# Table building of layer 0 queued behind the first norm's modulation, half of that norm's scaling on VectorE, byte masks

## The chip, the cores and the metric

The kernel runs on one core of a Trainium2 chip. The metric is device time in microseconds (us) of one execution; lower is better. Five engines work side by side, each through its own queue in a fixed order: TensorE (PE; its weight loads are shown as PEld), VectorE (DVE), ScalarE (ACT), GpSimd (POOL) and the queue engine SP, which issues most transfers (DMA).

## The reference

One inference step of a two-layer hybrid backbone on 128 context and 512 latent tokens of width 1024. For each layer:

```python
mod = silu(cond) @ w_mod + b_mod                 # sh1, sc1, g1, sh2, sc2, g2
h = rms_norm(x, norm1_g) * (1 + sc1) + sh1
aq, ak, av, bq, bk, bv, bg, br, cu, gz = split_cols(h @ w_in)
oa = diff_attention(...)                         # two softmax maps per head
ob = gla_chunked(...) forward and backward       # decays from br, gate bg
y_f, y_b = s5_scan(cu, lam, log_dt, b, c, h0)    # diagonal complex state space, both directions
oc = GLU(gelu(y_f + y_b + s5_d * cu))
x = x + g1 * ((sum of sigmoid(gz) * (branch @ w_branch)) @ w_out)
h = rms_norm(x, norm2_g) * (1 + sc2) + sh2
x = x + g2 * ((silu(h @ w_gate) * (h @ w_up)) @ w_down)
```

The state-space scan works in blocks of 8 tokens, for which tables of powers of its complex decays, multiplied into b and c, are built on the chip.

## The kernel before

The activations lie transposed, channels on partitions, 640 tokens along the free axis, in two halves of 320 (`hf`). A dense product splits both operands into a high and a low part, so each of its 128x128 blocks is three matmuls (`hh`,`whi`; `hl`,`whi`; `hh`,`wlo`). `wsplit` makes `whi` on ScalarE (L96, some on VectorE) and `wlo` on VectorE (L207). `dense_group` runs three weight columns over half 0, then lets `mid` prepare half 1, then runs them over half 1.

The kernel is written as one stream and a scheduler decides the order on each engine: an instruction that is ready early in the scheduler's own reckoning can be put ahead of one that was written earlier. `tc.issue_after(ins)` forbids this for what is traced inside it, on the engine of `ins` alone: these instructions stand behind `ins` in that engine's queue. It adds no wait.

The start of the program is what the change touches. `modulation(0, (1, 0))` computes the scale (round 1) and the shift (round 0) of the first norm from 16 weight loads of 512 KB (`wm`): matmuls L178, a transposition L187 (`last_mod`), and the additions of the bias into `M6` (L190). `nm0.stats(0)` sums squares, `nm0.apply(0)` makes, for each of 8 chunks, `nt = x * rstd` (L327), `nt = nt * a + sh` (L329), and the parts `hh` (L96) and `hl` (L331). Meanwhile `s5_tables(0)` (a generator, `t0`) builds the tables: a common part up to its first `yield`, then eight equal steps `e`, each with some 25 instructions on VectorE (phases L341 to L346 into `R`, factors into `FB`, L510 to L516), six products on GpSimd (`Wc`, `tm`, through `cmul` L341 to L346), transpositions and small matmuls on TensorE (L450, L458) and copies on ScalarE. `early()` writes step 0 and the statistics of half 1 in `first_tab`; the further steps stand between the gate products of `GLA_FILL`, and all eight are drained before the first linear-attention chunk. The block masks come as 512 KB of f32 and are cast to bytes on VectorE (L1228).

Of the kernel before, what the change touches and what calls it, by code (L numbers as in the profile page):

```python
# [10 lines left out]
F32 = mybir.dt.float32  # L11
# [3 lines left out]
AF = mybir.ActivationFunctionType  # L15
ALU = mybir.AluOpType
# [4 lines left out]
P = 128  # L21
# [17 lines left out]
    h="DADADADADADAAADADADADDDAAADADADADADADADADAAAAAAADDDADADAAAADDADA",  # L39
# [8 lines left out]
    a="AAAAAAAA",  # L48
    s="AAAAAAADAAAAAAADAAAAAAAAAAADADAAAAAAAADADAADAAAAAAAAADAAAAAAAAAADADAAAAAADAADAAAAAAAAADAAA"
       "AAAAAAAADADAAAAAADDDAAAAAAAAAAADAAAAADDAAAAAAAAAAAAAAA",  # L50
    r="AADAAAADAAAAAADADAAADAAAAADAAAAADAAADAAAAADAADAD",
# [4 lines left out]
    p="PPPDPPPPPDDDPPDPPPPPPDPDPPPPPDPP",  # L56
# [26 lines left out]
def tile_hybrid(ctx: ExitStack, tc: tile.TileContext, i: dict, o: dict):  # L83
    nc = tc.nc
    act, dve, pool, pe, sync = nc.scalar, nc.vector, nc.gpsimd, nc.tensor, nc.sync
# [8 lines left out]
    def copy(role, default, dst, src):  # L94
        e = eng(role, default)
        (e.copy if e is act else e.tensor_copy)(dst, src)  # L96
# [19 lines left out]
    def hs(hf):  # L116
        return slice(hf * HT, (hf + 1) * HT)
# [30 lines left out]
    masks = cp.tile([P, 8, P], U8, name="masks")  # L148
    rope = cp.tile([P, 2, NS], F32, name="rope")

    def V(l, name, j=0, n=1):
        b = VEC[name][0] + j
        return vec[:, l, b:b + n]
# [5 lines left out]
    dve.tensor_scalar(ctmp, ctmp, 0.5, 0.5, op0=ALU.mult, op1=ALU.add)  # L159
    dve.tensor_mul(scond[:, :, 0:2], ctmp, cond)  # L160

    M6s, mds, last_mod = {}, {}, [None]

    def modulation(l, rounds, mp=None):
        if l not in M6s:
            M6s[l] = cp.tile([P, 6, 2, 8], F32, name=f"M6_{l}")
            mds[l] = cp.tile([P, 4, 2, 8], F32, name=f"md_{l}")
        M6, md = M6s[l], mds[l]
        for r in rounds:
            mr = cp.tile([P, 256], F32, tag="mr", name=f"mr{l}_{r}", bufs=1)  # L170
            per = 8 if mp else 2
            for k0 in range(0, DC, per):
                pm = psd.tile([P, 512], F32, tag="d", name=f"pmod{l}_{r}_{k0}")
                for kc in range(k0, k0 + per):
                    wt = (mp or wp).tile([P, 4, 256], F32, tag="raw", name=f"wm{l}_{r}_{kc}", bufs=8 if mp else 3)
                    sync.dma_start(wt, i["w_mod"][l, r, kc])
                    for cg in range(4):
                        pe.matmul(pm[cg * 32:(cg + 1) * 32, 0:256], scond[:, kc, :], wt[:, cg, :],  # L178
                                  start=(kc == k0), stop=(kc == k0 + per - 1), tile_position=(0, cg * 32))
                if k0 == 0:  # L180
                    act.copy(mr, pm[:, 0:256])
                else:
                    dve.tensor_add(mr, mr, pm[:, 0:256])
                if k0 < DC - per:
                    yield
            for hf in range(2):
                last_mod[0] = pe.transpose(pm[:, 256 + hf * P:256 + (hf + 1) * P], mr[:, hf * P:(hf + 1) * P], ident)  # L187
            src = pm[:, 256:512].rearrange("p (h c s) -> p s c h", h=2, c=4)
            for s in range(2):
                dve.tensor_add(M6[:, r, s, :].rearrange("p (c h) -> p c h", h=2), src[:, s],  # L190
                               V(l, "bmod", r * 8, 8).rearrange("p (c h) -> p c h", h=2))
            if r in (1, 4):
                for s in range(2):
                    dve.scalar_tensor_tensor(md[:, r // 4, s, :], M6[:, r, s, :], 1.0,
                                             V(l, "n1g" if r == 1 else "n2g", 0, 8), op0=ALU.add, op1=ALU.mult)
            if r in (2, 5):
                dve.tensor_scalar_mul(md[:, 2 + r // 5], M6[:, r], 0.5)
            yield
# [49 lines left out]
    def dense(ap, xh, xl, fn):  # L248
        dense_mm(wload(ap, 1024), 0, list(range(8)), xh, xl, fn)

    def dense_group(pool_, items, xh, xl, pre, mid, ready=()):
        ws = list(ready) + [wload(ap, 1024, pool_ if ready or n < len(items) - 2 else None)
                            for n, (ap, fn) in list(enumerate(items))[len(ready):]]
        pre()
        for hf in range(2):
            for w, (ap, fn) in zip(ws, items):
                fn(hf, dense_half(w, 0, list(range(8)), xh, xl, hf))
            if hf == 0:
                mid()
# [39 lines left out]
    class Norm:  # L299
# [22 lines left out]
        def apply(self, hf):  # L322
            a, sh, tp, name = self.a, self.sh, self.tp, self.name
            hh, hl = self.h[0][hf], self.h[1][hf]
            for c in range(DC):
                t = tp.tile([P, HT], F32, tag="nt", name=f"nt{name}{c}{hf}", bufs=self.nb)
                dve.tensor_mul(t, self.x[:, c, hs(hf)], self.rs[hf])  # L327
                for s, sl in (((0, slice(0, NP)), (1, slice(NP, HT))), ((1, slice(0, HT)),))[hf]:
                    act.activation(t[:, sl], t[:, sl], AF.Identity, bias=sh[:, s, c:c + 1], scale=a[:, s, c:c + 1])  # L329
                copy("h", "DA"[c % 2], hh[:, c, :], t)  # L330
                self.last = dve.tensor_sub(hl[:, c, :], t, hh[:, c, :].bitcast(F32))  # L331
            if hf == 1:
                self.st.close()
# [525 lines left out]
    def run_layer(l, nm, mod, tabs, ffn_fill, after, ready=()):  # L859
# [14 lines left out]
        with ExitStack() as st:  # L874
# [13 lines left out]
            def cu_item(c, cpool=lp):  # L888
                cu = cpool.tile([P, 8, 81], F32, tag="G", name=f"cu{l}_{c}", bufs=3 if cpool is not lp else 2)
                pool.memset(cu[:, :, 16:17], 0.0)  # L890

                def cuf(hf, ps):
                    for a, b, n in (((0, 0, 16), (16, 17, 24)), ((0, 41, 40),))[hf]:
                        act.copy(cu[:, :, b:b + n].rearrange("p s n -> p n s"),
                                 ps[:, a * 8:(a + n) * 8].rearrange("p (n s) -> p n s", s=8))

                    if hf == 1:
                        pool.dma_start(u_d[:, c * P:(c + 1) * P, :].rearrange("s p n -> p s n"), cu)

                return ld(24 + c), cuf  # L900
# [59 lines left out]
            def point():  # L960
                todo(next(points))
# [11 lines left out]

            def early():
                def first_tab():
                    with tc.issue_after(last_mod[0].ins):
                        step("t0")
                    nm.stats(1)

                if l == 0:  # L980
                    with tc.tile_pool(name=f"cw{l}", bufs=1, reuse_waits="tile") as cw:
                        dense_group(cw, [cu_item(c, cw) for c in range(3)], hh, hl, first_tab, lambda: nm.apply(1), ready)
                    with tc.issue_after(nm.last.ins):
                        point()
                    ap, fn = cu_item(3)
                    dense(ap, hh, hl, fn)
                    point()
                else:
                    for c in range(4):
                        ap, fn = cu_item(c)  # L990
                        dense(ap, hh, hl, fn)
                        if c % 2:
                            point()
# [155 lines left out]
        with tc.tile_pool(name=f"fp{l}", bufs=1, reuse_waits="tile") as fp:  # L1149
            groups = [[0, 1]] + [list(range(2 + g * 4, 6 + g * 4)) for g in range(5)]  # L1150
            for gi, grp in enumerate(groups):
# [3 lines left out]
                for n, fc in enumerate(grp):  # L1155
                    t = fp.tile([P, T], F32, tag="ft", name=f"ft{l}_{fc}", bufs=2)
# [39 lines left out]
    def step(name, n=1):  # L1196
        for _ in range(n):
            next(gens[name], None)

    def drain(name):  # L1200
        for _ in gens[name]:
            pass

    def open_tabs(l):
        tb = tb_st.enter_context(tc.tile_pool(name=f"tb{l}", bufs=1, reuse_waits="tile", side="right"))
        gens[f"t{l}"] = s5_tables(l, tb, tabs)
# [7 lines left out]
    with tc.tile_pool(name="m0", bufs=1, reuse_waits="tile") as mp:  # L1214
        gens["m0a"] = modulation(0, (1, 0), mp)
        open_tabs(0)
        nm0 = Norm(x, None, None, "a0")
        nm0.stats(0)
        step("m0a")
        step("t0")  # L1220
        drain("m0a")
        ready = [wload(i["w_in"][0, 24 + c], 1024) for c in range(2)]
        rest_tabs(0)
        nm0.a, nm0.sh = mod_of(0)["a1"], mod_of(0)["sh1"]
        nm0.apply(0)
        mraw = mp.tile([P, 1024], F32, tag="raw", name="mraw", bufs=8)
        sync.dma_start(mraw, i["masks"])
        dve.tensor_copy(masks.rearrange("p a b -> p (a b)"), mraw)  # L1228
        sync.dma_start(rope, i["rope"])
    gens["m0b"] = modulation(0, (2, 4, 3, 5))  # L1230
    gens["m1"] = modulation(1, (1, 0, 2, 4, 3, 5))
# [45 lines left out]
def _prep(inp):  # L1277
    a = {k: np.asarray(v) for k, v in inp.items()}
    f = np.float32
    r = {}  # L1280
# [52 lines left out]
    for gi in range(6):  # L1333
        k0, k1 = max(0, gi * 4 - 2), gi * 4 + 2
        b = _blk(wd[:, k0 * P:k1 * P])
# [22 lines left out]
    for p in range(P):  # L1358
        d = p % 64
        hf, j = d // 32, d % 32  # L1360
# [4 lines left out]
    dm[:64, 0] = dm[:64, 17] = 0  # L1365
    dm[64:, 0] = dm[64:, 65] = 0
    r["dmask"] = dm
    return {k: np.ascontiguousarray(v) for k, v in r.items()}


# [26 lines left out]
```

## Time and profile before

| | us |
|---|---|
| median of 3 runs | 2774.8 (2773.85 to 2775.16) |
| profiled execution: span from first to last instruction | 2775.0 |
| busy in the span: PE / DVE / ACT / POOL | 2610.6 / 1692.5 / 868.1 / 393.7 |

The profiled execution's time is its span, 0.2 us above the median of the runs. Busy time counts an instruction from its start to its end, waits for a shared resource inside it included; a wait for a semaphore is idle time. The timeline counts from the start of the span.

### The profile page before, as it was taken

Reading aid. Unit: us, or ns where it says so; the run is one execution under the profiler, and the core shown is the slowest. Engines: PE = TensorE matmul, PEld = TensorE weight load, DVE = VectorE, ACT = ScalarE, POOL = GpSimd, SP = SyncE. Lnnn points to the kernel's source line nnn. Section 1 sums busy time; section 2 is a strip of 40 time slices with the busy share of each in tenths; the row PEclk is TensorE's granted clock in tenths of the full one; section 3 lists DMA queues with packets and bytes.
Section 4 is the critical chain, followed back from the end, with each engine's and each line's share of the span. In section 5 each row is a group of like instructions: output and inputs, shape, how many; then the busy total and the mean of one; then the engine's idle time right before and its main releaser. Section 6 shows DMA issues by size and latency. Waiting matters only on the chain. (4 is left out here: it accounts for less than half of the span.)

```text
span 2775.0 us, 45369 instructions
## 1 busy us (share of the span) xinstructions
PE 2610.6 (94%) x18528; PEld 2447.7 (88%) x18528; DVE 1692.5 (61%) x3563; ACT 868.1 (31%) x1617; POOL 393.7 (14%) x415
## 2 busy tenths in 40 slices
PE   4878989999999989999999999999999999999999
PEld 3866869988999979888999788899899999999999
DVE  8975667866544686675546635686764356434443
ACT  4433322255222431222214424223543233121211
POOL 3452021100211012121100201120111110000000
PEclk7889898999999999999999899999999999999999
DMA  6454244521113243354453122253211241222222
GB/s 254 138 189 151 73 147 135 154 72 40 56 54 120 67 133 131 126 191 153 136 166 112 59 75 67 88 157 106 64 44 58 72 137 43 76 77 77 77 76 77
DMA packets 123920, 293.47 MB, mean 106 GB/s; under 512 B 36256, under 2 KB 59808, under 8 KB 121664
## 3 DMA queue, kind: packets, MB, share of 16 engines
q1 hardware_dynamic: 116672, 248.59, 28.5%
q0 software_dynamic: 7040, 41.98, 4.1%
q8 instruction: 146, 2.39, 0.3%
q14 instruction: 62, 0.51, 0.1%
HBM read 252.12 MB, written 42.60 MB: 106 GB/s over the span
## 5 line engine op out<-in xcount | busy, mean ns | idle before, releaser
L207 DVE TENSOR_TENSOR wlo<-raw,whi 128x1024 fp32r<-128x1024 f32 (+1 forms) x306 | 365.4, 1195 | 387.5 <-ACT whi L96 386.4
L96 ACT CAST whi<-raw 128x1024 fp32r<-128x1024 f32 (+1 forms) x273 | 270.5, 993 | 699.3 <-PE pd L238 591.2
L238 PE MATMUL pd<-hh0a,whi 128*128 128x320 f32 x848 | 280.8, 332 | 7.7 <-DVE bg L663 2.0
L238 PE MATMUL pd<-hh0a,wlo 128*128 128x320 f32 x848 | 275.1, 325 | 11.6 <-DVE wlo L207 11.6
L238 PE MATMUL pd<-hl0a,whi 128*128 128x320 f32 x848 | 272.4, 322 | 3.9 <-DVE hl0a L331 3.9
L238 PE MATMUL pd<-hh1a,whi 128*128 128x320 f32 x848 | 265.5, 314 | 4.3 <-DVE qk L96 2.0
L238 PE MATMUL pd<-hl1a,whi 128*128 128x320 f32 x848 | 265.6, 314 | 0.0
L238 PE MATMUL pd<-hh1a,wlo 128*128 128x320 f32 x848 | 264.2, 312 | 0.0
L238 PE MATMUL pd<-hh0b,whi 128*128 128x320 f32 x704 | 221.4, 314 | 12.1 <-DVE ft L1160 7.8
L238 PE MATMUL pd<-ah,whi 128*128 128x320 f32 x704 | 221.0, 314 | 8.3 <-DVE x__2_8177 L337 2.0
L238 PE MATMUL pd<-hh1b,whi 128*128 128x320 f32 x704 | 218.7, 311 | 4.9 <-DVE ft L1160 4.9
L238 PE MATMUL pd<-hl0b,whi 128*128 128x320 f32 x704 | 219.3, 312 | 0.0
L238 PE MATMUL pd<-hh0b,wlo 128*128 128x320 f32 x704 | 219.1, 311 | 0.0
L238 PE MATMUL pd<-al,whi 128*128 128x320 f32 x704 | 218.5, 310 | 0.5 <-DVE al L207 0.5
L238 PE MATMUL pd<-ah,wlo 128*128 128x320 f32 x704 | 218.5, 310 | 0.2 <-DVE wlo L207 0.2
L238 PE MATMUL pd<-hh1b,wlo 128*128 128x320 f32 x704 | 218.3, 310 | 0.0
L238 PE MATMUL pd<-hl1b,whi 128*128 128x320 f32 x704 | 218.3, 310 | 0.0
L238 PEld LDWEIGHTS pd<-hh0a,whi 128*128 128x128 f32 x848 | 168.7, 199 | 17.9 <-issue 4.3
L238 PEld LDWEIGHTS pd<-hh0a,wlo 128*128 128x128 f32 x848 | 167.8, 198 | 16.1 <-DVE wlo L207 13.1
L238 PEld LDWEIGHTS pd<-hl0a,whi 128*128 128x128 f32 x848 | 168.6, 199 | 6.1 <-DVE hl0a L331 4.8
L238 PEld LDWEIGHTS pd<-hh1a,whi 128*128 128x128 f32 x848 | 161.5, 191 | 6.3 <-DVE qk L96 2.2
L238 PEld LDWEIGHTS pd<-hl1a,whi 128*128 128x128 f32 x848 | 161.2, 190 | 0.7 <-DVE hl1a L331 0.3
(515 smaller groups left out, 6065.8 us busy)
## 6 DMA issues: line engine op xcount, KB each, us to landing
raw<-in_w_in_dram SPq DMA_DIRECT2D x104, 512.0 KB, 3.7
wm<-in_w_mod_dram SPq DMA_DIRECT2D x96, 512.0 KB, 4.3
R_d<-R POOLq DMA_DIRECT2D x16, 1480.0 KB, 5.8
raw<-in_w_gate_dram SPq DMA_DIRECT2D x44, 512.0 KB, 3.6
raw<-in_w_up_dram SPq DMA_DIRECT2D x44, 512.0 KB, 3.5
raw<-in_w_down_dram SPq DMA_DIRECT2D x40, 512.0 KB, 3.5
raw<-in_w_branch_dram SPq DMA_DIRECT2D x24, 512.0 KB, 3.5
W<-R_d SPq DMA_DIRECT2D x16, 512.0 KB, 3.6
```

Source lines behind the costliest of these rows:

```text
L96: (e.copy if e is act else e.tensor_copy)(dst, src)
L207: dve.tensor_sub(lo, src, hi.bitcast(F32))
L238: pe.matmul(ps[:, :HT], ww, xx[hf][:, kc, :], start=(n == 0 and j == 0), stop=(n == last and j == 2))
```

## The change

Three edits. `modulation` also keeps its last addition on VectorE (`last_add`), and step 0 of the tables is traced inside an `issue_after` for it, beside the one for TensorE: on VectorE step 0 now stands behind the addition that completes the first norm's shift. In `apply`, for this norm's half 0 alone, the four odd chunks are scaled by a VectorE `tensor_scalar` (two each, of 128 and 192 elements) in place of two ScalarE activations. The masks are an input of bytes and go to their tile directly.

```diff
-    M6s, mds, last_mod = {}, {}, [None]
+    M6s, mds, last_mod, last_add = {}, {}, [None], [None]
...
-                dve.tensor_add(M6[:, r, s, :].rearrange("p (c h) -> p c h", h=2), src[:, s],
+                last_add[0] = dve.tensor_add(M6[:, r, s, :].rearrange("p (c h) -> p c h", h=2), src[:, s],
                                V(l, "bmod", r * 8, 8).rearrange("p (c h) -> p c h", h=2))
...
-                    act.activation(t[:, sl], t[:, sl], AF.Identity, bias=sh[:, s, c:c + 1], scale=a[:, s, c:c + 1])
+                    if name == "a0" and hf == 0 and c % 2:
+                        dve.tensor_scalar(t[:, sl], t[:, sl], a[:, s, c:c + 1], sh[:, s, c:c + 1], op0=ALU.mult, op1=ALU.add)
+                    else:
+                        act.activation(t[:, sl], t[:, sl], AF.Identity, bias=sh[:, s, c:c + 1], scale=a[:, s, c:c + 1])
...
-                    with tc.issue_after(last_mod[0].ins):
+                    with tc.issue_after(last_mod[0].ins), tc.issue_after(last_add[0].ins):
                         step("t0")
                     nm.stats(1)
...
-        mraw = mp.tile([P, 1024], F32, tag="raw", name="mraw", bufs=8)
-        sync.dma_start(mraw, i["masks"])
-        dve.tensor_copy(masks.rearrange("p a b -> p (a b)"), mraw)
+        sync.dma_start(masks.rearrange("p a b -> p (a b)"), i["masks"])
...
+    r["masks"] = r["masks"].astype(np.uint8)
```

VectorE's queue before, around the two pairs of additions into `M` (L190); `R`, `tp`, `tm`, `FB`, `tv` are the tables' tiles, `E` their powers, and the second L190 pair is the one that the norm needs:

```order
L190 TENSOR_TENSOR M_0_164<-pmod_1_0_167,vec 128x8 x2
L194 SCALAR_TENSOR_TENSOR md_165<-M_0_164,vec 128x8
...
L513 TENSOR_TENSOR R_0_533<-bc_0_227,PP_371 128x4x160
L514 TENSOR_TENSOR tv_0_571<-bc_0_227,PP_371 128x640
L341 TENSOR_TENSOR R_1_923<-E_0_341,E_0_318 64x4x64
L516 SCALAR_TENSOR_TENSOR R_0_533<-R_0_533,tv_0_571 128x4x160
L344 TENSOR_TENSOR R_1_923<-E_0_341,E_0_318 64x4x64
L341 TENSOR_TENSOR R_1_923<-E_0_341,E_0_318 64x4x64
L344 TENSOR_TENSOR R_1_923<-E_0_341,E_0_318 64x4x64
L190 TENSOR_TENSOR M_0_164<-pmod_0_0_383,vec 128x8 x2
L207 TENSOR_TENSOR wlo_440<-raw_437,whi_439 128x1024
```

The same place in the changed program (L330 is the new scaling, line numbers after it are three higher):

```order
L349 TENSOR_TENSOR E_0_364<-E_0_364,tt_294 128x32
L190 TENSOR_TENSOR M_0_164<-pmod_1_0_167,vec 128x8 x2
L194 SCALAR_TENSOR_TENSOR md_165<-M_0_164,vec 128x8 x2
L881 TENSOR_SCALAR hv_507<-vec 128x8
L883 TENSOR_SCALAR lt_506<-vec 128x1
L190 TENSOR_TENSOR M_0_164<-pmod_0_0_383,vec 128x8 x2
L330 TENSOR_SCALAR nta_456<-nta_456,md_165,M_0_164 128x128
...
L330 TENSOR_SCALAR nta_492<-nta_492,md_165,M_0_164 128x192
L344 TENSOR_TENSOR R_0_531<-E_0_341,E_0_318 64x4x64
L345 TENSOR_TENSOR tp_0_532<-E_0_341,E_0_318 64x256
```

Between the two pairs of L190 there were 29 rows, 25 of them of step 0 and of the start of step 1; now there are three, of four short instructions. The first table row stands behind the norm's first half.

TensorE's queue before, from the modulation's transposition to the first dense products, and behind the third column's products (`pd_711`) over half 0:

```order
L187 MATMUL pmod_0_0_383<-ident,mr_0_382 128x128 x2
L450 MATMUL pwt_0_578<-ident,Wc_0_564 128x128 x8
L458 MATMUL pk_0_589<-R_0_533,FB_0_555 32x128 x16
L238 MATMUL pd_657<-hh0a_114,whi_439 128x320
...
L450 MATMUL pwt_1_968<-ident,Wc_1_954 128x128 x8
L458 MATMUL pk_1_979<-R_1_923,FB_1_945 32x128 x16
L289 MATMUL npsa_634<-ident,rsmna_640 128x64 x5
```

The changed program at the same two places (the third column is `pd_709` here, L453 and L461 are the former L450 and L458):

```order
L187 MATMUL pmod_0_0_383<-ident,mr_0_382 128x128 x2
L238 MATMUL pd_655<-hh0a_114,whi_439 128x320
...
L238 MATMUL pd_709<-hh0a_114,wlo_528 128x320
L453 MATMUL pwt_0_576<-ident,Wc_0_562 128x128
...
L270 MATMUL npsa_632<-avg,nacca_609 64x1 x5
L453 MATMUL pwt_1_966<-ident,Wc_1_952 128x128 x3
L289 MATMUL npsa_632<-ident,rsmna_638 128x64 x5
```

Step 0's TensorE work moved from ahead of the 72 dense products of half 0 to behind them; step 1's remains ahead of half 1 in part. From table step 4 on (VectorE's `tm<-PW,FB`, TensorE's gate products) the queues of all engines are the same in both programs.

## Rows read from the trace of the kernel before

**Rows 1.** The page: its span, and the engines' busy time and share.

```profile
span 2775.0 us, 45369 instructions
PE 2610.6 (94%) x18528; PEld 2447.7 (88%) x18528; DVE 1692.5 (61%) x3563; ACT 868.1 (31%) x1617; POOL 393.7 (14%) x415
```

**Rows 2.** Stretches: length; PE, PEld, DVE, ACT, POOL busy; clock; DMA share; GB/s.

```profile
40.00:50.00 10.00, 3.27 (x40) 2.19 (x40) 8.53 (x10) 2.59 (x4) 6.60 (x5) 0.50 0.17 68
50.00:60.00 10.00, 8.86 (x36) 8.23 (x37) 10.00 (x23) 10.00 (x25) 4.60 (x8) 0.60 0.31 107
80.00:90.00 10.00, 8.78 (x46) 8.49 (x47) 9.82 (x27) 7.81 (x19) 0.04 (x1) 0.74 0.33 131
120.00:140.00 20.00, 16.92 (x151) 15.64 (x151) 19.28 (x38) 8.89 (x27) 6.10 (x8) 0.83 0.38 143
140.00:190.00 50.00, 33.93 (x271) 27.99 (x269) 48.12 (x68) 12.69 (x37) 29.60 (x24) 0.81 0.44 162
190.00:200.00 10.00, 10.00 (x65) 10.00 (x66) 2.33 (x5) 3.58 (x9) 3.32 (x6) 0.95 0.56 205
```

**Rows 3.** Timeline of DVE: start, duration, instruction, idle time before it.

```profile
29.13 0.41 DVE L341 TENSOR_TENSOR R<-E,E 64x256 f32<-64x256 f32 x1
30.39 0.23 DVE L190 TENSOR_TENSOR M<-pmod,vec 128x8 f32<-128x8 f32 x2
31.20 0.20 DVE L346 TENSOR_TENSOR E<-E,tt 128x32 f32<-128x32 f32 x1
...
47.20 0.24 DVE L190 TENSOR_TENSOR M<-pmod,vec 128x8 f32<-128x8 f32 x2
48.87 1.23 DVE L207 TENSOR_TENSOR wlo<-raw,whi 128x1024 fp32r<-128x1024 f32 x1 [1.42 <-ACT whi L96]
```

**Rows 4.** Timeline of PE: the modulation's transposition, the first dense products.

```profile
36.62 0.69 PE L187 MATMUL pmod<-ident,mr 128*128 128x128 f32 x2 [0.55 <-ACT mr L181]
50.48 0.87 PE L238 MATMUL pd<-hh0a,whi 128*128 128x320 f32 x2 [1.08 <-DVE hh0a L96]
```

**Rows 5.** Timeline of ACT behind the second pair of additions.

```profile
47.41 0.49 ACT L329 ACTIVATE nta<-nta,M,md 128x128 f32<-128x128 f32 x1 [10.84 <-DVE M L190]
47.81 1.03 ACT L96 CAST whi<-raw 128x1024 fp32r<-128x1024 f32 x1
```

**Rows 6.** Timeline of DVE: instructions that give prices.

```profile
17.50 0.17 DVE L407 TENSOR_SCALAR cs<-cs 128x32 f32<-128x32 f32 x1
...
40.43 1.67 DVE L514 TENSOR_TENSOR tv<-bc,PP 128x640 f32<-128x640 f32 x1
42.03 1.48 DVE L341 TENSOR_TENSOR R<-E,E 64x256 f32<-64x256 f32 x1
...
50.01 0.32 DVE L96 CAST hh0a<-nta 128x320 fp32r<-128x320 f32 x1
51.39 0.48 DVE L331 TENSOR_TENSOR hl0a<-nta,hh0a 128x320 fp32r<-128x320 f32 x1
53.51 1.70 DVE L1228 CAST masks<-mraw 128x1024 uint8<-128x1024 f32 x1
...
67.61 0.81 DVE L514 TENSOR_TENSOR tv<-bc,PP 128x640 f32<-128x640 f32 x1
```

**Rows 7.** Timeline of POOL: third product of step 0, first of step 1.

```profile
39.79 1.63 POOL L344 TENSOR_TENSOR Wc<-PW,FB 128x512 f32<-128x512 f32 x1
...
53.41 1.10 POOL L341 TENSOR_TENSOR Wc<-PW,FB 128x512 f32<-128x512 f32 x1 [3.67 <-DVE FB L343]
```

**Rows 8.** Waits of PE from 120 to 190 us: total, times, longest.

```profile
PE pd L238 <- DVE wlo L207: 7.8, 1, 7.8
```

**Rows 9.** Timeline of PE: dense products at either level of its clock.

```profile
69.25 0.47 PE L238 MATMUL pd<-hh0a,whi 128*128 128x320 f32 x1
69.52 0.47 PE L238 MATMUL pd<-hl0a,whi 128*128 128x320 f32 x1
95.12 0.31 PE L238 MATMUL pd<-hh0a,wlo 128*128 128x320 f32 x1
95.27 0.30 PE L238 MATMUL pd<-hh0a,whi 128*128 128x320 f32 x1
```

## The prediction

> **What bounds the kernel now.** The page comes first: TensorE is busy 94% of a span of 2775.0 us, VectorE 61% [rows 1]. That average hides the start. The table of stretches shows it: from 50 to 190 us VectorE is busy nearly without a break (10.00 of 10, 9.82 of 10, 19.28 of 20, 48.12 of 50), while TensorE has holes (33.93 of 50 from 140 to 190); only from 190 us on is it the other way round, VectorE 2.33 of 10 and TensorE 10.00 [rows 2]. What opens TensorE's largest hole there is VectorE: 7.8 us for one `wlo` [rows 8]. So up to 190 us the time is set by how soon VectorE is through its queue, which is the eight table steps, the norm and the weight splits; from there on TensorE carries whatever delay it has to the end. For an edit in this stage the question is not when TensorE may start, but whether VectorE stands idle longer or does more.
>
> The timeline of VectorE shows where it idled. From 29.13 to 47.20 us it works on table step 0 and the first of step 1, with the first pair of L190 between; then come the second pair of L190, a wait of 1.42 us for `whi`, and the first `wlo` [rows 3]. The second pair could have run far earlier: TensorE ended the transposition for it at 36.62 + 0.69 = 37.31 us [rows 4]. ScalarE waits 10.84 us for these additions, and the first dense product comes at 50.48 [rows 4, 5]. That is the wait which the first edit takes away.
>
> **The change, part by part.**
>
> *Step 0 behind the norm.* The additions move from 47.20 to about 37.35 us, 9.85 us earlier, and the first dense product with them, to about 41. That is TensorE's gain at this place. VectorE's side is a loss. After 29.13 us it has left, ahead of the additions: four small instructions on `E` of about 0.2 us, each waiting for the one before (0.9 us together, by the 0.20 of the last), the first L190 pair (0.23), two of about 0.16 behind it and two still smaller ones; by some 1.5 us in all it is done at 30.6 [rows 3], as the changed queue above lists them. Nothing else may go ahead of the additions, and TensorE's part of the modulation, up to 37.31, is not touched by any edit. **VectorE idles 37.35 - 30.6 = 6.7 us** (6.2 to 7.0), in time that it filled with table work before. The table work is not gone: it stands behind the norm's first half.
>
> *The wait for `whi`.* ScalarE's first scaling began 0.21 us after the additions and its first `whi` 0.40 us later, taking 1.03 [rows 3, 5]: the same sequence ends near 37.35 + 0.21 + 0.40 + 1.03 = 39.0. VectorE now has six scalings to do first, until about 38.3. The 1.42 us [rows 3] become 0.7 (0.1 to 1.2): **-0.7 us**.
>
> *The masks.* An instruction starts about 0.09 us before the one ahead ends (48.87 + 1.23 = 50.10, the cast behind it at 50.01 [rows 3, 6]), so the masks' cast of 1.70 us takes 1.6 of VectorE's queue. A GpSimd product that ended at 53.41 + 1.10 = 54.51 us was then running [rows 7], so part of that was waiting, which another instruction now takes: between 0.6 (55.21 - 54.51 - 0.09) and 1.6, I take **-1.1 us**. The transfer shrinks from 512 to 128 KB, behind the weights of the modulation in the queue; from 40 us on the transfers' share is 0.17 [rows 2], so nothing waits for it.
>
> *Scaling on VectorE.* Eight instructions of 128 and 192 elements that the trace does not have. The nearest rows, each less 0.09: a `tensor_scalar` of 32 elements, 0.08 us, from below; the two-tensor L331 of 320 elements, 0.39, from above; a cast of 320 elements between them, 0.23 [rows 6]. Half the cast's elements and one input tensor speak for the lower half: 8 x 0.14 = **+1.1 us** (0.6 to 3.1). The page "VectorE: DVE Perf Modes" of the Trainium skill (section on mode 2x_2P) says that a one-tensor f32 instruction within SBUF gives two results a cycle; with its fixed 58 cycles (section on the errata) an estimate is 4 x (0.13 + 0.16) = 1.2 us, and the sum would be the same within 0.1. ScalarE loses eight activations; it is not what VectorE waits for afterwards, so that counts nothing.
>
> *New waits.* Step 0's tail now meets the statistics of half 1. In TensorE's queue the transposition that hands the statistics back (L289) stands behind three transpositions of step 1, which need GpSimd's products; VectorE's queue has two instructions that wait for TensorE close by. Each was free before. **+1.0 us** (0 to 3) for them together.
>
> *The shared resource.* While GpSimd runs a product, a VectorE instruction takes until its end and then its own time: L514 1.67 us beside one, 0.81 alone; L341 1.48 against 0.41 [rows 3, 6]; the product of 39.79 + 1.63 = 41.42 ends 0.68 us before that L514 does [rows 7]. The same six products of step 0 now run some 20 us later, against the same kind of instructions: 0, with 2 us either way.
>
> From table step 4 on all queues are as before, so the delay is a pure shift from there. VectorE's 1.88 us without work from 140 to 190 [rows 2] can absorb at most that: **-0.5 us**.
>
> Sum: 6.7 - 0.7 - 1.1 + 1.1 + 1.0 - 0.5 = **+6.5 us**. The profiled time is 2775.0, the median of the runs 2774.8; they agree within 0.2 us, so the prediction is 2774.8 + 6.5 = **2781.3 us**, slower by 0.23%. What a measurement of this kernel can tell from no change is about 0.2%, 5.5 us.
>
> **Rivals.**
>
> *Tables are not the bound (faster).* If VectorE has slack of more than 6.7 us between 50 and 190 us, the idle time is made up there and the early start stays: 9.85 us at most, 2765. For it: TensorE did have nothing to do from 43 to 50 us but step 0's small matmuls (3.27 us busy of 10 from 40 to 50). Against it: 48.12 of 50 us busy, and 7.8 us of TensorE waiting for a `wlo` that stood behind tables [rows 2, 8]. It decides if VectorE's unoccupied time from 50 to 190 us exceeds the loss; the stretches shown leave 2.8 us (0.18 + 0.72 + 1.88).
>
> *The loss is paid back by the shared resource (no change).* From 29.13 to 47.20 us GpSimd's products stretched VectorE's instructions by about 0.9 us each where they met (1.67 against 0.81, 1.48 against 0.41). If the six products of step 0 now fall where VectorE waits anyway, up to 6 x 0.9 = 5.4 us come back: 2776. Against it: in the new order too they run beside two-tensor work of step 0 and the statistics.
>
> *TensorE's clock (more).* Its early block is followed by a long pause until step 0's products are done, over 10 us. The granted clock was 0.50 from 40 to 50 us, after a stretch with little work, and 0.74 from 80 to 90 [rows 2]; at the lower level (1.2 GHz) a dense product follows the last by 0.27 us, at the upper (2.4) by 0.15 [rows 9]. Half 1 has 72 of them; some half ran at the lower level, and if all do, 36 x 0.12 = 4.3 us more stand between the norm and the next weights, whose `whi` needs a buffer that these products hold: 2786. That a pause lets the clock fall is also what the page "TensorE: Matmul & The Clock Gate" of the Trainium skill says (Part 1: slow by default, released by activity); the 0.50 after the modulation agrees.
>
> **Chances.** The forecast (2779 to 2785) 0.55; more than that, by the clock or dear scalings, 0.12; paid back, 0.26; faster, 0.07. Slower by over 0.2% (above 2780.3): 0.48 of the forecast's and 0.12, 0.60; within 0.2%: 0.07 and 0.26, 0.33; faster: 0.07. The bounds of the terms added up go from 0 (6.2 - 1.3 - 1.6 + 0.6 + 0 - 1.9 - 2) to +14 (7.0 - 0.2 - 0.6 + 3.1 + 3 + 0 + 2). The range 2776 to 2788 leaves out the faster case, the lowest of the paid-back one and the clock's worst.
>
> **What would show it.** Right: in the changed profile the second pair of L190 at 37 to 38 us with 6 to 7 us idle ahead of it; the first dense product near 41; the first table phase on VectorE near 46; VectorE nearly without a break from there to about 196, and its first long idle 6 to 7 us later than 190. Wrong: if VectorE shows idle stretches between 50 and 190 us beyond those waits and reaches table step 4 no later, the tables did not bind; if TensorE's clock is at 0.5 through half 1's products, the last rival holds; if the additions stay late, the queue was not what held them.

## The result and the profile after

The changed kernel takes 2793.91 us (median of four runs, 2789.32 to 2797.28); the kernel before took 2774.98 in the runs beside it. The ratio is 1.0051, with a 95% interval from 1.0032 to 1.0071: slower, by more than the forecast 6.5 us and outside its range. In the later comparisons the kernel before had medians of 2781.1 to 2785.7 us, so of the 19 us between the two medians (the ratio makes it 14) a part is spread between executions; the control run below shows where the spread lies. The comparison of the traces therefore keeps to the first 220 us, which repeat to 0.3 us.

The page of the changed kernel, the lines that answer [rows 1]:

```profile
span 2789.4 us, 45366 instructions
PE 2611.1 (94%) x18528; PEld 2444.5 (88%) x18528; DVE 1696.1 (61%) x3570; ACT 864.0 (31%) x1609; POOL 391.1 (14%) x415
```

TensorE's work is the same within 0.5 us: the time is in its pauses. The stretches of the changed kernel, columns as in [rows 2]:

```profile
40.00:50.00 10.00, 9.43 (x48) 9.01 (x48) 9.91 (x25) 7.54 (x23) 0.00 (x0) 0.72 0.49 151
60.00:70.00 10.00, 4.04 (x47) 3.13 (x45) 8.09 (x20) 1.43 (x3) 3.55 (x5) 0.50 0.37 152
70.00:80.00 10.00, 0.48 (x1) 0.18 (x1) 9.94 (x18) 0.83 (x5) 8.75 (x7) 0.50 0.04 12
80.00:90.00 10.00, 9.36 (x47) 7.43 (x48) 9.65 (x25) 7.81 (x17) 0.22 (x1) 0.68 0.00 0
140.00:190.00 50.00, 36.21 (x299) 31.42 (x299) 47.96 (x81) 15.88 (x47) 23.82 (x23) 0.86 0.42 160
190.00:200.00 10.00, 4.94 (x45) 3.52 (x42) 9.97 (x9) 0.56 (x2) 8.61 (x5) 0.78 0.66 226
```

TensorE has its early block from 40 us and then little to do from 60 to 80 us, while VectorE is busy for 8.09 and 9.94 of the 10 us. The last row shows the delay at its end: where VectorE had been free from 190 us on [rows 2], it is now busy for 9.97 of the 10 us. The timeline of VectorE around the second addition pair, the answer to [rows 3]:

```profile
36.52 0.24 DVE L190 TENSOR_TENSOR M<-pmod,vec 128x8 f32<-128x8 f32 x2 [6.01 <-PE pmod L187]
36.72 1.73 DVE L330 TENSOR_SCALAR nta<-nta,md,M 128x128 f32<-128x128 f32 x6
38.36 1.22 DVE L207 TENSOR_TENSOR wlo<-raw,whi 128x1024 fp32r<-128x1024 f32 x1
...
43.98 0.35 DVE L330 TENSOR_SCALAR nta<-nta,md,M 128x128 f32<-128x128 f32 x1
...
44.65 0.38 DVE L330 TENSOR_SCALAR nta<-nta,md,M 128x192 f32<-128x192 f32 x1
44.94 0.41 DVE L344 TENSOR_TENSOR R<-E,E 64x256 f32<-64x256 f32 x1
```

The pair comes 10.7 us earlier with 6.01 us of idle time ahead of it, `wlo` follows without the 1.42 us of waiting, and the first table phase begins at 44.94. The early dense product of [rows 4] now starts at 39.97 us. What VectorE waited for between 30 and 132 us (total, times, longest):

```profile
DVE M L190 <- PE pmod L187: 6.0, 1, 6.0
DVE wlo L207 <- ACT whi L96: 1.3, 1, 1.3
DVE Z L467 <- ACT Z L466: 1.0, 2, 0.8
DVE rsmna L275 <- PE npsa L270: 1.0, 1, 1.0
```

Before, the same view from 30 to 120 us has one row, 1.7 us for `whi`. To see what was not waiting, take the stretch from 30 us to the instruction that begins VectorE's own products of table step 4 (`tm<-PW,FB`, 119.00 us before, 131.06 after). First the kernel before, then the changed one:

```profile
30.00:119.00 89.00, 65.24 (x457) 56.70 (x458) 86.30 (x168) 40.55 (x100) 43.23 (x41) 0.77 0.45 155
```

```profile
30.00:131.06 101.06, 64.75 (x450) 54.90 (x451) 90.52 (x173) 36.02 (x90) 41.73 (x42) 0.74 0.40 132
```

The stretch is 12.1 us longer: 7.8 us of it idle (10.54 against 2.70) and 4.2 us busy. Eight scalings came in and one cast went, worth about +2.2 and -1.6 us (two small table instructions fell behind the mark); the other 3.6 us are instructions that take longer than they did. The two longest of them, in VectorE's timeline, took 2.5 and 4.0 us more than such an instruction takes alone (0.82 and 0.21), so the ordinary meetings with GpSimd together cost less than before:

```profile
100.42 3.32 DVE L516 TENSOR_TENSOR R<-bc,PP 128x640 f32<-128x640 f32 x1
...
106.67 4.21 DVE L344 TENSOR_TENSOR FB<-bc,f 128x64 f32<-128x64 f32 x1
110.80 0.21 DVE L345 TENSOR_TENSOR tm<-bc,f 128x64 f32<-128x64 f32 x1
```

and GpSimd's timeline beside the second:

```profile
106.51 0.94 POOL L901 DMA_DIRECT2D u_d<-cu  x1 [3.46 <-ACT cu L897]
107.47 1.29 POOL L346 TENSOR_TENSOR Wc<-Wc,tm 128x512 f32<-128x512 f32 x1
108.72 1.06 POOL L347 TENSOR_TENSOR Wc<-PW,FB 128x512 f32<-128x512 f32 x1
109.73 1.05 POOL L348 TENSOR_TENSOR tm<-PW,FB 128x512 f32<-128x512 f32 x1
```

An instruction of 64 elements that takes 0.21 us (the row behind it) took 4.21, until all three products had ended at 110.78. The prediction had let such an instruction wait for one product.

### The profile page after: what moved, and what is told of

It is laid out like the page before. It is cut to its first block, busy times and chain, and to the rows that moved or that the text cites. A ratio compares the mean times of both kernels' runs of the same rounds, so it can differ in the third digit from the quotient of the medians.

```text
span 2789.4 us, 45366 instructions
## 1 busy us (share of the span) xinstructions
PE 2611.1 (94%) x18528; PEld 2444.5 (88%) x18528; DVE 1696.1 (61%) x3570; ACT 864.0 (31%) x1609; POOL 391.1 (14%) x415
## 5 line engine op out<-in xcount | busy, mean ns | idle before, releaser
L238 PE MATMUL pd<-hh0a,wlo 128*128 128x320 f32 x848 | 274.1, 323 | 10.5 <-DVE wlo L207 10.5
L238 PE MATMUL pd<-hh0b,whi 128*128 128x320 f32 x704 | 221.6, 315 | 12.1 <-DVE ft L1163 7.9
L238 PEld LDWEIGHTS pd<-hh0a,wlo 128*128 128x128 f32 x848 | 167.0, 197 | 14.6 <-DVE wlo L207 11.7
```

The lines of the kernel that those rows point to most:

```text
L238: pe.matmul(ps[:, :HT], ww, xx[hf][:, kc, :], start=(n == 0 and j == 0), stop=(n == last and j == 2))
```

## The experiments

**The theories.** A: VectorE's queue is the bound up to 200 us, and the change costs there the time that VectorE idles and the time that it loses to GpSimd's products. Against it stand B, that the scalings are what costs, and C, that TensorE's clock behind its early block does. H, formed later, says which meetings with GpSimd are dear: those of a VectorE instruction that begins while GpSimd issues a transfer, and is then held through the products behind it. Three marks serve for comparison: VectorE's step 4 (119.00 us before), the end of the tables, which is GpSimd's first transfer into `M_d` (197.81), and VectorE's first scan of the linear attention (212.54). In the changed kernel they lie at 131.06 (+12.1), 209.92 (+12.1) and 225.89 (+13.4).

**Control: the kernel before again** (no edit).

> The kernel before once more, as a control of what one trace can tell. If the order of the queues alone sets the first 200 us, VectorE reaches table step 4 within 0.5 us of 119.00 us; what differs behind 200 us between two traces of the same kernel (up to 5 us in the traces so far) is then spread, not the change.

Measured: 119.06, 198.09 and 212.72 us, against a span of 2795.3 us. The first 220 us repeat; behind them the same kernel lost 20 us. The profile shows the granted clock lower there in this execution: 0.88 against 0.96 from 540 to 620 us, 0.94 against 0.98 from 890 to 1040. So a lone difference behind 220 us says nothing, and the marks say more than one time does.

**The queue edit alone.**

```diff
...
-                    with tc.issue_after(last_mod[0].ins):
+                    with tc.issue_after(last_mod[0].ins), tc.issue_after(last_add[0].ins):
```

> The queue edit alone; scaling on ScalarE and f32 masks as before. Theory A (VectorE's queue is the bound: it idles 6.0 us ahead of the second addition pair, and step 0's GpSimd products then meet its work longer): the changed kernel reaches table step 4 on VectorE 12.1 us late (131.06 against 119.00 us); without its scalings (2.2 us in its trace) and with the masks' cast (1.6 us in the trace of before) this kernel should be 11.4 us late there, and its time 2785 to 2791 us. Theory B (the eight scalings on VectorE are what costs, by where they stand between the norm's steps): this kernel loses the idle time alone, 6 us at most, 2778 to 2781. Theory C (TensorE's clock after its early block): the early block and the pause are here too, so the time is that of the changed kernel, 2789 to 2797, and the granted clock is 0.5 behind the block.

Measured: 128.73 (+9.7), 208.58 (+10.8) and 225.27 (+12.7) us; median 2794.09, ratio 1.0038 (1.0018 to 1.0059). Theory B is out: without a single scaling most of the loss at step 4 (9.7 of 12.1 us) is there. The median lies above what A expected (2785 to 2791) and where C did, but the kernel before was 6 us slower in this comparison too; between A and C this run does not decide. The idle time ahead of the second pair is that of the changed kernel, and one instruction, of 0.8 us alone, takes 4.4 us longer; these two, 10.4 us, account for the 9.7 at step 4:

```profile
36.73 0.24 DVE L190 TENSOR_TENSOR M<-pmod,vec 128x8 f32<-128x8 f32 x2 [5.99 <-PE pmod L187]
...
100.47 5.23 DVE L513 TENSOR_TENSOR R<-bc,PP 128x640 f32<-128x640 f32 x1
```

**The scalings alone**, and **the byte masks alone.**

```diff
+                    if name == "a0" and hf == 0 and c % 2:
+                        dve.tensor_scalar(t[:, sl], t[:, sl], a[:, s, c:c + 1], sh[:, s, c:c + 1], op0=ALU.mult, op1=ALU.add)
...
```

> The eight scalings on VectorE alone; queue and masks as before. Theory A: VectorE is full from 47 us on, so their 2.2 us (0.28 each in the trace of the changed kernel) come out as delay, less what VectorE waits for the copies of ScalarE: 0 to +2.2 us at table step 4 and in the time, 2775 to 2777. Theory B: more than 4 us late, 2779 or more. Theory C: no difference, within 1 us of before.

```diff
...
-        dve.tensor_copy(masks.rearrange("p a b -> p (a b)"), mraw)
+        sync.dma_start(masks.rearrange("p a b -> p (a b)"), i["masks"])
...
```

> The byte masks alone. Theory A: the cast's 1.6 us of VectorE's queue are gone and table step 4 comes 0.6 to 1.6 us earlier, time 2773 to 2775. Theory B and theory C: the same, since neither speaks of the masks; if the time is over 1 us longer, theory A is wrong on what a free microsecond of VectorE is worth there.

The scalings: step 4 at 121.24 (+2.2), the end of the tables at 200.26 (+2.5), the scan at 215.92 (+3.4); ratio 1.0004 (0.9982 to 1.0026). The bytes: 119.58 (+0.6), 198.39 (+0.6), 213.93 (+1.4); ratio 0.9997 (0.9974 to 1.0020). Neither can be told from no change by its time. That the bytes gained nothing although the cast was gone is a miss of what theory A expected, and VectorE's timeline shows where the 1.6 us went:

```profile
95.43 4.30 DVE L341 TENSOR_TENSOR R<-E,E 64x256 f32<-64x256 f32 x1
```

This phase takes 0.41 us alone [rows 3]; with the queue moved by the cast's time it met a GpSimd transfer issue at 95.22 and the products behind it. A saving on VectorE is not worth its length where the new place of the next instruction decides what it meets.

**Step 0 split**: its phases, factors and GpSimd's products may go ahead of the second addition pair, only the rest is held behind it; byte masks, scaling on ScalarE.

```diff
...
+            if l == 0 and e == 0:
+                yield
...
                     with tc.issue_after(last_mod[0].ins):
                         step("t0")
+                        with tc.issue_after(last_add[0].ins):
+                            step("t0")
```

> The queue edit for the second half of step 0 alone (its Vc products L513 to L519 and its tail), with byte masks: the phases, the factors and GpSimd's products of step 0 may stand ahead of the second addition pair, some 20 instructions and 7 us that fit where the changed kernel idles 6.0 us. Scaling stays on ScalarE. Theory A: the idle time ahead of the pair falls from 6.0 to under 1.5 us, the first dense product still comes near 42 us, GpSimd's products of step 0 run from 37 to 47 us; VectorE reaches table step 4 within 3 us of before, and the time is 2771 to 2778. Theory C: the early block of dense products and the pause behind it are the same as in the changed kernel, so the clock falls to 0.5 behind it too and the time stays 2785 or more.

Measured: the pair at 40.03 us with no wait ahead of it, the first dense product at 46.12 (not 42: VectorE's queue ahead of the pair is longer than I had put it), step 4 at 120.91 (+1.9), the scan at 214.73 (+2.2); ratio 1.0003 (0.9981 to 1.0025). TensorE's clock falls here too, to 0.50 from 70 to 80 us, and 11.2 us of the loss at the scan are gone, so the clock alone does not cost them. The pause is a shorter one than in the changed kernel (5.72 us busy in these 10 against 0.48), and this run by itself does not put theory C to the full test; what does is the list of waits above, where of VectorE's 10.5 us of idle time at most 3.3 (`Z` and `rsmna` 1.0 each, the later `whi` 1.3) can come from a slower TensorE. But the early start brings nothing either: filled again, VectorE is where it was.

**All products of layer 0 on VectorE**, in the kernel before, in the changed one, and in the split one. In `C` each letter stands for three products, two letters for a table step; P is GpSimd, D VectorE.

```diff
-    C="PPPPPPPPDPPPPPPPPPPPPPPPPPPPPPPP",
+    C="DDDDDDDDDDDDDDDDPPPPPPPPPPPPPPPP",
```

> The kernel before with all products of layer 0's tables on VectorE instead of GpSimd (45 products of 128x512, 0.6 us each on VectorE, which takes 0.68 for one at 118.14 us). Theory A (while GpSimd runs a product, VectorE's instructions are held up; the excess over their durations alone adds up to 39 us from 30 to 200 us, 0.86 for each product): VectorE gives 45 x 0.6 = 27 us and gets 39 back, so it comes to the end of the tables 8 to 12 us earlier, and the time is 4 to 12 us shorter than that of before. Rival (the long instructions are long for another reason, and GpSimd's products are free work): VectorE is 27 us later and the time 20 us longer or more.

> The changed kernel with the same products on VectorE. Theory A: without GpSimd's products nothing stretches and nothing waits for them, so against the kernel before with the same edit only the idle time ahead of the second addition pair (6.0 us), the scalings (2.2), the masks (-0.7 to -1.6) and the wait for the low part (-1.4) are left: 4 to 7 us later at table step 4 and in the time, in place of 12. If the 12 us stay, GpSimd's products have no part in the loss.

> Step 0 split as in the run with the split (phases, factors, products ahead of the second addition pair, the rest behind), byte masks, and the products on VectorE. Theory A: no idle time over 1.5 us ahead of the pair, no stretch and the early first product: within 2 us of the kernel before with the products on VectorE, and shorter than the kernel before by 4 to 12 us. If the order of step 0 matters by itself, it differs from that one by more than 4 us.

GpSimd's timelines at the end of the tables, for the kernel before, the changed kernel, and the two with the products on VectorE (of before, then of the changed one):

```profile
197.81 5.01 POOL L528 DMA_DIRECT2D M_d<-Z_d  x8 [5.03 <-DMA Z_d<-Z]
```

```profile
209.92 5.00 POOL L531 DMA_DIRECT2D M_d<-Z_d  x8 [5.04 <-DMA Z_d<-Z]
```

```profile
187.88 4.99 POOL L528 DMA_DIRECT2D M_d<-Z_d  x8 [7.08 <-DMA Z_d<-Z]
```

```profile
193.89 5.00 POOL L531 DMA_DIRECT2D M_d<-Z_d  x8 [6.14 <-DMA Z_d<-Z]
```

At the end of the tables the change costs 12.1 us with the products on GpSimd and 6.0 without (at the scan 13.4 and 5.7; between the medians of the two with the products on VectorE 4.2). These runs split the loss: half of it goes with GpSimd's products, and theory A's 4 to 7 hold for the rest. That the rest is the idle time ahead of the pair and the scalings less the cast (6.3 + 2.2 - 1.6 us) fits but is not shown term by term: without the products on GpSimd VectorE also has other idle time up to its last table instruction, 10.5 us in the kernel before and 9.0 in the changed one. The first of these two also shows what the products cost in the kernel before. The stretch from 30 to 200 us, before and then with the products on VectorE:

```profile
30.00:200.00 170.00, 127.09 (x948) 111.16 (x949) 157.00 (x277) 65.71 (x170) 83.20 (x79) 0.80 0.45 160
```

```profile
30.00:200.00 170.00, 116.32 (x885) 98.11 (x878) 141.94 (x321) 63.70 (x166) 18.91 (x38) 0.77 0.49 166
```

VectorE did 44 instructions more, of about 0.6 us each in its queue, and was busy for 15 us less. The tables ended 9.9 us earlier, as expected, but the time did not follow: the scan came 10.3 us late, and the ratio was 1.0006 (0.9985 to 1.0028), a miss. The waits of TensorE from 120 to 215 us begin with:

```profile
PE pwt L450 <- DVE Wc L343: 13.0, 3, 5.4
PE pk L458 <- DVE R L516: 5.3, 3, 3.7
PE pd L238 <- ACT mg__1_514 L886: 5.2, 2, 5.0
```

Now TensorE stands at transpositions that wait for products low in VectorE's queue, with dense work behind them; that place had waited 9 us for GpSimd and VectorE together before. The changed kernel with this edit has the ratio 1.0023 (1.0008 to 1.0039). The split one was expected within 2 us of the unsplit and ended its tables 3.7 us later (191.59; ratio 1.0024, 1.0006 to 1.0042): the order of step 0 matters even without GpSimd.

**Some of the products on VectorE.** Steps 0, 1 and 7 (first line), also 5 and 6 (second), in both with the three of step 4 that VectorE had before on GpSimd; and in the split kernel the second half of steps 1 and 2 (third), or of every step (fourth).

```diff
-    C="PPPPPPPPDPPPPPPPPPPPPPPPPPPPPPPP",
+    C="DDDDPPPPPPPPPPDDPPPPPPPPPPPPPPPP",
...
+    C="DDDDPPPPPPDDDDDDPPPPPPPPPPPPPPPP",
...
+    C="PPPDPDPPPPPPPPPPPPPPPPPPPPPPPPPP",
...
+    C="PDPDPDPDPDPDPDPDPPPPPPPPPPPPPPPP",
```

> The kernel before with the products of table steps 0, 1 and 7 on VectorE (18) and the others on GpSimd (30, of which step 4's first three were VectorE's before). With all of them on VectorE the tables ended 10 us earlier, but TensorE then waited for products and for gates (13.0 us for one kind of transposition alone from 120 to 215 us). Theory A: moving only those at the start, where VectorE's queue is the bound, and at the end keeps the gain: each product moved frees 0.86 - 0.6 = 0.26 us, about 4 us in all at the end of the tables and 2 to 6 us in the time. If the interleaving of the queues decides and not the held-up VectorE, TensorE is later at 220 us although the tables end earlier.

> As the run with steps 0, 1 and 7 on VectorE, with steps 5 and 6 there too (30 products in all). Theory A: the tables end some 7 us earlier than before and the time is 2 to 7 us shorter. If the interleaving decides, the steps at the end make TensorE wait for the products as in the run with all of them on VectorE (10 us late at 220 us), and this kernel is slower than before.

> The split of step 0 and the byte masks, with the second three products of steps 1 and 2 on VectorE and step 4's on GpSimd. It was 2.2 us late at 220 us with GpSimd's products as before. Theory A: the 3 us of new waits (for the first tables' transpositions and the statistics, 1.36 and 0.99) shrink as step 1's products come sooner; within 3 us of before at 220 us, and time within 0.2% of before. Against the changed kernel 10 us shorter.

> The split of step 0 and the byte masks, with three of the six products of every step on VectorE. Theory A: 24 products moved free 24 x 0.26 = 6 us and no step hands GpSimd six products in a row, so the longest stretch (3.3 and 4.2 us in the changed kernel) falls under 2.5 us; the tables end 6 us earlier than before, and the time is 0 to 6 us shorter. If the interleaving decides, TensorE is later than before at 220 us.

| products on VectorE | end of tables | scan | median | ratio (95%) |
|---|---|---|---|---|
| steps 0, 1, 7 | 199.17 (+1.4) | 208.59 (-4.0) | 2773.41 | 0.9958 (0.9939 to 0.9978) |
| steps 0, 1, 5, 6, 7 | 189.48 (-8.3) | 221.53 (+9.0) | 2777.06 | 0.9974 (0.9956 to 0.9991) |
| split, half of 1 and 2 | 204.54 (+6.7) | 217.15 (+4.6) | 2785.47 | 0.9988 (0.9969 to 1.0006) |
| split, half of all | 198.33 (+0.5) | 218.47 (+5.9) | 2785.64 | 0.9996 (0.9979 to 1.0013) |

The kernel before stood at 2785.68 in these comparisons. The first row beats both kernels: it is 0.42% (0.22 to 0.61) faster than the one before. Its products of steps 0 and 1 take 0.69 us each on VectorE, where GpSimd takes 1.10 and 1.63 for two of them [rows 7] and holds VectorE up beside. Its tables do not end earlier, against the expectation; the first dense product comes at 47.34 us in place of 50.48. The split kernels missed theirs: where two kinds of products share a step, VectorE and TensorE wait for the other half (TensorE 10.3 us for `Wc` from GpSimd and 7.3 for `Wc` from VectorE in the last one, from 60 to 225 us), as the rival of the interleaving said; the longest VectorE instruction did fall to 2.2 us there. The second row is faster than before too (by 0.26%, 0.09 to 0.44) with a scan that comes 9.0 us late; the marks don't explain it, and why the first gains 12 us where the scan gains 4 is open too.

**What makes a meeting dear**: the stores of the tables and of `u_d` issued from ScalarE's queue instead of GpSimd's, in the changed kernel, in the one before and in the fastest; and the fastest one's edit in the changed kernel.

```diff
-            pool.dma_start(R_d[e], R)
+            (act if l == 0 else pool).dma_start(R_d[e], R)
...
-            pool.dma_start(Z_d[gs].rearrange("g i c -> (g i) c"), Z)
+            (act if l == 0 else pool).dma_start(Z_d[gs].rearrange("g i c -> (g i) c"), Z)
...
-                        pool.dma_start(u_d[:, c * P:(c + 1) * P, :].rearrange("s p n -> p s n"), cu)
+                        (act if l == 0 else pool).dma_start(u_d[:, c * P:(c + 1) * P, :].rearrange("s p n -> p s n"), cu)
```

> The changed kernel with layer 0's stores of the tables and of the scan's input issued from ScalarE's queue instead of GpSimd's. Theory H (a VectorE instruction that begins while GpSimd issues a transfer is held through the products that follow it): no VectorE instruction of the first 210 us takes over 3 us (three did, 3.32, 4.21 and 4.07), and those held by products take at most one or two products' time. Rival (back-to-back products alone hold VectorE for that long): instructions of over 3 us are there as before. The time is no test, since ScalarE's queue now waits where it issues: 2780 to 2800 us.

> The kernel before with the same stores issued from ScalarE's queue. Theory H: its one instruction of over 3 us (4.06) is gone. Rival: it is still there. Against this kernel the changed one with the same edit should be later by 6 to 9 us in place of 12 if the long holds are a good part of the excess, since it loses three of them and this one a single one.

> The fastest kernel so far (products of steps 0, 1 and 7 on VectorE) with the stores issued from ScalarE's queue. Theory H: its long holds (4.07, 2.85 and 2.00 us) shrink to under 2 us, 4 us for VectorE; whether the time gains as much depends on what ScalarE's queue waits for: 2765 to 2780.

> The changed kernel with the products of steps 0, 1 and 7 on VectorE. The idle time of 6.0 us stays, but step 0's and step 1's products no longer meet VectorE, so against the same edit of the kernel before (2.2 to 6 us shorter than before at 220 us) it should be 5 to 8 us later at 220 us, not 12 to 13; the time within 0.3% of the kernel before.

Theory H's first part holds: without issues on GpSimd no VectorE instruction of the first 210 us takes over 2.3 us, in none of the three. The longest pair of the changed kernel with this edit, which does begin beside products that follow one another, is

```profile
115.67 4.29 DVE L207 TENSOR_TENSOR wlo<-raw,whi 128x1024 fp32r<-128x1024 f32 x2
```

two instructions of 1.2 us each alone (38.36, above) in 4.29. Its second part, that the long holds are what the change costs, can't be read from these runs: ScalarE's queue now stands still where it issues, and the edit cost the kernel before itself 0.69% (0.39 to 1.00), the changed one 0.52% (0.28 to 0.76) against the unedited kernel before. In the kernel before VectorE now waits 22.7 us for `whi` from ScalarE between 30 and 225 us, where it had waited 11.7; in the changed one that wait is 10.7, and what holds it up instead was not looked into. Their scans lie at 225.40 (changed) and 228.74: the change comes 3.3 us early there, where it was expected 6 to 9 us late. The fastest kernel lost its lead by it (ratio 1.0009, 0.9986 to 1.0032), a miss of the 2765 to 2780. With steps 0, 1 and 7 on VectorE the changed kernel ends its tables at 204.02, 4.9 us behind the same edit of before, but its scan at 217.78 is 9.2 us behind, not 5 to 8; ratio to before 1.0000 (0.9977 to 1.0023). One wait of TensorE, from 60 to 225 us, is new there and may be the difference:

```profile
PE pla L553 <- DMA wa<-in_wa_dram: 4.7, 1, 4.7
```

a transfer of weights for which TensorE waited 1.5 us at most in the other kernels. Why it came late is not shown.

## Why the prediction was wrong

The direction was right, and so was the mechanism of the idle time: the second pair at 36.5 us with 6 us idle ahead of it, the first dense product near 40, the first table phase at 44.94 (46 was forecast), VectorE nearly full to 200 us. The size was half, mostly because the other part of the loss, the meetings with GpSimd, had been put at nothing. Term by term, to table step 4:

- *Idle ahead of the second pair*, +6.7 (6.2 to 7.0): measured 6.01. Right, if just below its bounds; the pair came at 36.52 and not 37.35, since the transposition it waits for ended at 36.41 in this trace.
- *The wait for `whi`*, -0.7: the `wlo` came without a wait, -1.42.
- *The masks*, -1.1: the cast's 1.6 us went, and alone it left step 4 0.6 us later.
- *The scalings*, +1.1: 1.73 + 0.35 + 0.38 us in the rows above, 2.2 with the overlaps taken off, and +2.2 alone at step 4. The lower half of my bounds was the wrong half. The estimate of 1.2 by the page "VectorE: DVE Perf Modes" of the Trainium skill (mode 2x_2P with the errata's fixed part of 58 cycles) does not fit: the six in a row took 0.29 us each. The same section says that this fixed part under-predicts and that about 150 cycles were measured; an estimate with those is 4 x (0.22 + 0.26) = 1.9 us, nearer.
- *New waits*, +1.0: `Z` and `rsmna` waited 1.0 us each. To that come 1.3 us for a later `whi`, 1.0 more than before; 3.0 together, the upper bound of the term. The later `whi` has the form of the clock rival (it waits for half 1's products, at a granted clock of 0.68 from 80 to 90 us against 0.74 before), at a price of at most 1 us and not 4.3; what part of it is the clock is not shown.
- ***The shared resource*, 0 with 2 either way: this step failed.** It rested on the sentence that a VectorE instruction takes until the end of one product and then its own time. Instructions grew by 3.6 us to step 4, because two were held through two and three products; and with the products off GpSimd in both kernels the change costs 6.0 us instead of 12.1. That this is close to the 6.5 of the sum is in part luck: the sum's other terms missed by -0.7, -0.7, -0.5, +1.1 and +2.0, and those kernels have idle time of their own.
- *Absorbed later*, -0.5: nothing was; +12.1 at step 4 became +13.4 at the scan.

The measured terms add up to 11.8 of the 12.1 us (6.0 - 1.4 - 1.6 + 2.2 + 3.0 + 3.6). The loss at the marks lies inside the bounds of the terms added up, 0 to +14; the forecast had given a time above its 2785 us, 10.2 more than before, a chance of 0.12.

The rival that the shared resource pays the loss back went the other way in sum: the ordinary meetings did become cheaper, by some 3 us (3.6 less the 6.5 of the two long holds), but the long holds cost more than that. That the tables are not the bound is refuted up to 200 us by the queue edit alone. The clock did fall, to 0.50 (the 1.2 GHz level) from 60 to 80 us behind TensorE's early block, but VectorE was busy 8.09 and 9.94 of 10 us in it and waited 1.8 us in all for what TensorE makes (`rsmna` 1.0, and 0.8 for a `Z` that ScalarE copies), so its price there is 1.8 us at most. The distance from 13.4 us at the scan to the 19 between the first medians I put down to spread, by the control's 20 us; that is argued, not shown. For it speaks the queue edit alone, 12.7 us late at the scan and 13.0 in its median of 12 runs beside 35 of the kernel before.

The page "SBUF — State Buffer" of the Trainium skill (section "SBUF: two separate sides") says that the port pair which VectorE and GpSimd share is an exclusive lock: of a VectorE instruction with two inputs in SBUF and a GpSimd instruction, whichever starts first has it for the whole instruction, and the other fully blocks. The single meetings agree (1.67 against 0.81 us in [rows 6]); the 4.21 us do not follow from it, since by the trace VectorE's instruction began at 106.67, ahead of the products at 107.47, 108.72 and 109.73, and ended behind all three.

## What to carry to other kernels

Where an engine is the bound, ask of a reordering first what that engine does in the time that comes free: here it idled 6 us for another engine's early start that nobody needed. When work moves against a neighbour that shares a resource, "the same meetings elsewhere" is not zero: price it by the dearest meeting that the trace shows (the kernel before had one, 4.06 us at 141.23, that the prediction left out), not by the typical one. And look whether the helper pays at all: GpSimd's 45 products up to 200 us took 1.06 to 1.98 us, held VectorE up beside, and on VectorE took 0.69; with 18 or 30 of them on VectorE the kernel was faster than before, with all of them it was not.

## What the runs showed of the hardware

In 18 traces, 14 VectorE instructions of the first 210 us took over 3 us (3.32 to 5.23, of 0.2 to 1.2 alone), and all 14 began while GpSimd was issuing a transfer of its own that table products followed within 0.1 us (in one of them behind a second issue); with the issues moved to ScalarE there were none. They were held through two to four products, the 5.23 us of the queue edit alone the longest. Such an issue is not enough: of some 70 VectorE instructions that began within one, 46 took under 1 us. In the kernel before, one of 0.82 us began at 158.59 within an issue (158.28 to 158.83) and ran its usual time, and a phase like the one that took 4.30 us with the byte masks began at 96.09 within an issue (96.06 to 96.95) and took 0.41. What decides between the two is open.
